# One transformer block on one core: a new order of the second product's seven partial products, five pairs of split weight tiles, and the residual added piece by piece

## The chip, the cores and the metric

The kernel runs on one core of a Trainium2 chip. The metric is the device time of one execution in microseconds (us); lower is better. A core has five engines that work through their own queues in order: TensorE (PE) multiplies matrices, VectorE (DVE) and ScalarE (ACT) do elementwise work, GpSimd (POOL) does a little of it here, and SyncE (SP) issues nearly all DMAs. Tiles lie in the on-chip memory SBUF, matmul results in the accumulator memory PSUM, which has eight banks.

## The reference

`x` is 512 rows of 2048 columns, all float32. After the attention part, the block computes a two-layer MLP with a residual:

```
x  = x + concat(headnorm(oa), headnorm(ob)) @ W_out
h2 = rmsnorm(x, g_mlp)
u  = relu(h2 @ W_up)                # W_up: 2048 x 8192
x  = x + (u * u) @ W_down           # W_down: 8192 x 2048
y  = rmsnorm(x, g_final)
```

The change lies in the lines from `W_out` on. Everything ahead of them (input projection and two kinds of attention) is left as it is.

## The kernel before, in words

**Split products.** Every float32 product is made of three matmuls (`mm3`): each operand is split into a rounded high part and a low rest, and high times high, high times low and low times high are added up. The split of a weight tile (`split`, L58 to L61) is an ACT copy that makes the high part (`wh`, L60) and a DVE subtraction that makes the low part (`wl`, L61). `hi_lo` hands out the tiles for both; there are three such pairs, handed out in turn, so a split of a fourth tile waits until PE has done with the first.

**Seven products instead of eight.** Both MLP products are computed in blocks of two by two with seven partial products each, numbered 1 to 7. Their operands are sums and differences of the blocks. On the weight side, DVE makes them in place, each from the one ahead: product 5 uses b12-b11, product 6 uses b22 minus that, product 4 uses b21 minus the operand of 6, and product 7 uses b22-b12. So product 6's operand can be made only when product 5's has been split, and so on.

**Attention output (L456 to L481).** For four column quarters `n`, PE computes `acco`; DVE adds it to `x` (L469), ACT sums the squares (L471), PE transposes, ACT scales into `hr` (L478), and `a_form` makes the seven activation operands from it and splits them into `F[p]` (tiles `fh`, `fl`).

**Up stage (32 `Unit`s).** A unit loads two raw weight tiles `wu` (pool `rw`, five buffers), makes and splits the seven operands and computes the products into three accumulators (`psa`, `psb`, `psc`), 24 matmuls a product. Products 3 and 4 of a unit run inside the next unit. After two units `store_form` makes the seven activation operands for the second product, one after each product of the loop, splits them into a staging tile `st` (two buffers) and writes them to DRAM (`ufd`).

**Down stage.** The first 30 units are read back in groups (the first of two units, seven of four). For each group and each column half `db`, four raw tiles `wd` are loaded and seven products of 12 matmuls per two units are computed, each into one of two `accd` accumulators or, for product 1, into `m`, which stays in PSUM. DVE then adds `accd` to a running sum in SBUF (L653). The residual `x` is read into four of the sums ahead of the first group and scaled there (L659 to L662). The last two units are multiplied without the seven-product scheme (`acce`), with the final norm.

**Order.** The program order is that of the code, changed by a scheduler that moves instructions of each engine by estimated times; the hardware then runs each queue strictly in the built order. SP's queue is one of them: a DMA whose buffer is not free yet holds up all DMAs behind it.

Of the kernel before, what the change touches and what calls it, by code (L numbers as in the profile page):

```python
# [8 lines left out]
F32 = mybir.dt.float32  # L9
# [26 lines left out]
def block_kernel(ctx, tc, x, g_attn, w_in, b_f, g_out_sb, g_out_fox, w_out, g_mlp, w_up, w_down, g_final, y):  # L36
# [392 lines left out]
    F = {p: tuple(form.tile([P, KC // 2, 2 * P], F32R, tag=f"f{c}{p}", name=f"f{c}{p}") for c in "hl") for p in range(1, 8)}  # L429
    xp_cm = tc.tile_pool(name="xp", bufs=1, reuse_waits="tile")  # L430
# [20 lines left out]
    for n in range(4):  # L451
# [32 lines left out]
    xp_cm.__exit__(None, None, None)  # L484
    trp_cm.__exit__(None, None, None)
    acc_cm.__exit__(None, None, None)

    v2 = cp.tile([P, TB], F32, name="v2")
    dve.tensor_reduce(v2, ss2, axis=mybir.AxisListType.X, op=ALU.add)
    dve.tensor_scalar(v2, v2, 1.0 / D, EPS, op0=ALU.mult, op1=ALU.add)  # L490
    ev = cp.tile([P, TB], F32, name="ev")
    dve.scalar_tensor_tensor(ev, v2, EPS, v2, op0=ALU.mult, op1=ALU.mult)
# [4 lines left out]
    sg_cm = tc.tile_pool(name="sg", bufs=2, reuse_waits="tile")  # L497
    sg = sg_cm.__enter__()
    ups_cm = tc.tile_pool(name="ups", bufs=1, space=PSUM, reuse_waits="tile")
    ups = ups_cm.__enter__()  # L500
    GROUPS = [(0, 2)] + [(u, 4) for u in range(2, NU - 2, 4)]
    ufd = {}
    for u0, n in GROUPS:
        t_ = {p: dp.tile([P, 2, n, 2 * P], F32, name=f"ufd{p}_{u0}") for p in range(1, 8)}
        for j in range(0, n, 2):
            ufd[u0 + j] = {p: t_[p][:, :, j:j + 2, :] for p in t_}
            ufd[u0, n] = t_
    usd = [dp.tile([P, 2, 2, NT], F32, name=f"usd{u}") for u in range(2)]

    class Unit:  # L510
        def __init__(self, u):
            self.u = u
            cols = slice(2 * u * P, 2 * (u + 1) * P)
            rows_ = w_up.rearrange("(a i p) f -> i p a f", i=2, p=P)
            if u == 0:

                self.b = [[wp.tile([P, KC // 2, P], F32, tag="wraw", name="wq") for _ in range(2)] for _ in range(1)]
                for j in range(2):
                    sp.dma_start(self.b[0][j], rows_[0][:, :, j * P:(j + 1) * P])
# [6 lines left out]
            self.A, self.B, self.C = (ups.tile([P, NT], F32, tag=c, name=f"ps{c}", bufs=n)[:, :2 * P]  # L526
                                      for c, n in (("a", 3), ("b", 2), ("c", 3)))
            if u % 2 == 0:
                hidden[0] = sg.tile([P, 2, 2, NT], F32, tag="c", name="c")
            self.pair = hidden[0]  # L530
            self.c = hidden[0][:, u % 2]

        def product(self, p):
            (b11, b12), (b21, b22) = self.b
# [14 lines left out]
            if p in (1, 6, 7):  # L549
                self.m = sg.tile([P, 2 * P], F32, tag=f"m{p}", name=f"s{p}")  # L550
# [16 lines left out]
    def store_form(p, c, dst):  # L567
        st = sg.tile([P, 2, 2, 2 * P], F32R, tag="st", name="st")
        a_form(p, c, (st[:, 0], st[:, 1]))
        sp.dma_start(dst, st.bitcast(F32))  # L570

    hidden = {}
    todo = []
    old = None
    for u in range(NU + 1):
        new = Unit(u) if u < NU else None
        for who, p in ((new, 1), (old, 4), (new, 5), (new, 6), (old, 3), (new, 2), (new, 7)):
            if who is None:
                continue
            who.product(p)  # L580
            if todo:
                store_form(*todo.pop(0))
            if p == 3 and who.u % 2 == 1 and who.u < NU - 2:
                todo += [(q, who.pair, ufd[who.u - 1][q]) for q in A_ORDER]
        old = new
    for u in range(2):
        for h in range(2):
            st = sg.tile([P, 2, NT], F32R, tag="st", name="su")
            split(st[:, 0], st[:, 1], hidden[0][:, u, h])
            sp.dma_start(usd[u][:, :, h, :], st.bitcast(F32))  # L590
    sg_cm.__exit__(None, None, None)
    ups_cm.__exit__(None, None, None)


    SUM_AT = {2: 1, 4: 5, 7: 6, 3: 2, 5: 7, 6: 4}
    UF_AT = {1: 1, 2: 5, 5: 6, 6: 2, 4: 7, 7: 4, 3: 3}
    ORDER = (1, 2, 5, 6, 4, 7, 3)
    QUADS = [[2, 3], [4, 7]]
    M = {p: form.tile([P, 2, 2, NT], F32, tag=f"fl{SUM_AT[p]}", name=f"m{p}") for p in SUM_AT}
# [3 lines left out]

    sp_ = ctx.enter_context(tc.tile_pool(name="spare", bufs=1, reuse_waits="tile"))
    dps_cm = tc.tile_pool(name="dps", bufs=2, space=PSUM, reuse_waits="tile")
    dps = dps_cm.__enter__()
    mps_cm = tc.tile_pool(name="mps", bufs=1, space=PSUM, reuse_waits="tile")
    mps = mps_cm.__enter__()
    M1 = [mps.tile([P, 2, NT], F32, name=f"m1{db}") for db in range(2)]
    uf = {}  # L610
# [5 lines left out]
    def load_b(group, db):  # L616
        u0, n = group
        rows_ = w_down[2 * u0 * P:2 * (u0 + n) * P].rearrange("(u s p) c -> s p u c", s=2, p=P)
        b = []
        for j in range(2):  # L620
            for s in range(2):
# [6 lines left out]
    def product(p, b, db, n, first):  # L628
        b11, b21, b12, b22 = b
# [10 lines left out]
        for u0 in range(0, n, 2):  # L640
            hi, lo = (w.rearrange("p (a b) -> p a b", a=2) for w in hi_lo(2 * NT))
            split(hi, lo, src[:, u0:u0 + 2, :])
            for t in range(2):
                ts = slice(t * P, (t + 1) * P)
                for u in range(2):
# [4 lines left out]
        if first and p in (5, 6):  # L650
# [4 lines left out]
    for p in ORDER:  # L655
        load_uf(p, GROUPS[0])
    for p, t0, j in ((2, 0, 0), (4, 1, 0), (7, 1, 1), (3, 0, 1)):
        for db in range(2):
            sp.dma_start(M[p][:, :, db, :], xd[2 * j + db][:, 2 * t0:2 * t0 + 2, :])  # L659
# [4 lines left out]
    ws, us, late = {}, [None, None], []  # L664
# [13 lines left out]
    def in_spare(tag):  # L678
        return lambda shape, name: sp_.tile(shape, F32R, tag=tag, name=name)

    def last_hidden(u, at_):
        t_ = at_([P, 2, 2, NT], f"us{u}")
        sp.dma_start(t_.bitcast(F32), usd[u])
        us[u] = (t_[:, 0], t_[:, 1])

    for g, group in enumerate(GROUPS):
        for db in range(2):
            if g == len(GROUPS) - 1 and db == 1:
                last_hidden(0, in_spare("us0"))
                last_weights(0, [in_spare("ws0"), in_spare("ws1")])  # L690
            b = load_b(group, db)
            for p in ORDER:
                product(p, b, db, group[1], g == 0)
                if db == 1 and g < len(GROUPS) - 1:
                    load_uf(p, GROUPS[g + 1])
    last_low = lows[0]
    last_hidden(1, in_form(1))
# [6 lines left out]
    def last_product(t, n, pool_, tag):  # L704
        ts = slice(t * P, (t + 1) * P)
        ps = pool_.tile([P, NT], F32, tag=tag, name="acce")
        for i in range(4):
            wh, wl = ws[n, i // 2]
            mm3(ps, *(h[:, i % 2, ts] for h in us[i // 2]), wh[:, i % 2, :], wl[:, i % 2, :], i == 0, i == 3)
        ins = dve.tensor_tensor(x2(t, n), x2(t, n), ps, op=ALU.add)  # L710
        junk = sp_.tile([P, NT], F32, tag="junk", name="junk3")
# [87 lines left out]
```

## Time and profile before

| | |
|---|---|
| median of 3 runs | 2134.7 us (2134.11 to 2135.95) |
| the profiled execution's own time | 2133.93 us |
| its span, first to last instruction | 2132.2 us |
| PE busy | 2088.0 us (98%) |
| DVE busy | 1572.0 us (74%) |
| ACT busy | 1019.6 us (48%) |
| mean granted clock of TensorE | 0.996 of full speed |

The profiled execution is 1.7 us longer than its span and 0.8 us below the median. Busy times of PE are made of modelled ends: a matmul of the up stage is shown 0.28 us long though the next one starts 0.12 us after it, so a wait looks shorter by the difference than it is.

### The profile page before, as it was taken

What the parts mean: (1) busy time and instruction counts of PE and PEld (TensorE: products, weight loads), DVE (VectorE), ACT (ScalarE), POOL (GpSimd) and SP (SyncE); (2) the same over time, 40 slices, a digit from 0 to 9 for tenths busy, and PEclk for the clock granted to TensorE, in tenths of its full rate; (3) what the DMA queues carried; (4) which work ended last, traced back from release to release, by engine and by line L of the source; (5) the groups of instructions that cost most, each with busy time, mean ns of one, the idle gap of its engine ahead of it and who ended that gap; (6) DMA issues with size and microseconds to landing.
All of it is one profiled execution on the core that took longest, in us unless ns stands there. A gap on an engine that the chain in (4) does not pass through costs nothing.

```text
span 2132.2 us, 29833 instructions
## 1 busy us (share of the span) xinstructions
PE 2088.0 (98%) x12084; PEld 1844.9 (87%) x12084; DVE 1572.0 (74%) x1729; ACT 1019.6 (48%) x1366; POOL 53.3 (2%) x75
## 2 busy tenths in 40 slices
PE   8999999999999999999999999999999999999998
PEld 8888887888898888999999999999778788788786
DVE  5454546665666667888888888888888878878887
ACT  5333334444445554556556556557433333333443
POOL 0000000000010000000000000000000000000004
PEclk9999999999999999999999999999999999999999
DMA  6323323323324434555656655567954564664631
GB/s 188 80 89 80 89 79 79 85 74 89 80 80 138 139 129 147 169 181 185 205 176 200 202 187 188 185 215 276 341 202 174 217 226 160 224 227 151 239 117 79
DMA packets 237354, 339.68 MB, mean 159 GB/s; under 512 B 7792, under 2 KB 150688, under 8 KB 230048
## 3 DMA queue, kind: packets, MB, share of 16 engines
q1 hardware_dynamic: 236256, 335.64, 47.7%
q8 instruction: 95, 1.56, 0.3%
q10 hardware_dynamic: 960, 2.13, 0.3%
q14 instruction: 43, 0.35, 0.0%
HBM read 272.20 MB, written 65.54 MB: 158 GB/s over the span
## 4 chain that ended last, share of the span: by engine, by line
PE 87%; DVE 6%; ACT 3%; DMA 3%; issue 1%; SPq 0%; ACTq 0%; DVEq 0%
PE accd L88 6%; PE accd L89 6%; PE accd L87 6%; PE accq L87 5%; PE accq L89 5%; PE accq L88 5%; PE psa L87 5%; PE psa L88 5%; PE psa L89 5%; PE acco L87 3%; PE acco L88 3%; PE acco L89 3%; PE psc L87 3%; PE psc L88 3%; PE accv L87 3%; PE accv L88 3%
## 5 line engine op out<-in xcount | busy, mean ns | idle before, releaser
L60 ACT CAST wh<-wd 128x1024 fp32r<-128x1024 f32 x210 | 219.7, 1054 | 338.4 <-PE accd L89 237.8
L61 DVE TENSOR_TENSOR wl<-wu,wh 128x1024 fp32r<-128x1024 f32 x220 | 267.8, 1222 | 72.5 <-ACT wh L60 72.4
L61 DVE TENSOR_TENSOR wl<-wd,wh 128x1024 fp32r<-128x1024 f32 x210 | 253.7, 1221 | 85.3 <-ACT wh L60 85.3
L60 ACT CAST wh<-wu 128x1024 fp32r<-128x1024 f32 x220 | 228.6, 1046 | 170.2 <-PE psa L88 63.1
L88 PE MATMUL accd<-wl,uf 128*128 128x512 f32 x720 | 282.5, 392 | 13.2 <-DVE wl L61 13.2
L87 PE MATMUL psa<-fh,wh 128*128 128x256 f32 x1024 | 291.3, 285 | 3.5 <-ACT s L551 2.4
L88 PE MATMUL psa<-fl,wh 128*128 128x256 f32 x1024 | 290.8, 284 | 0.0
L89 PE MATMUL psa<-fh,wl 128*128 128x256 f32 x1024 | 289.8, 284 | 0.0
L87 PE MATMUL accd<-wh,uf 128*128 128x512 f32 x720 | 279.0, 391 | 3.1 <-ACT wh L60 2.5
L89 PE MATMUL accd<-wh,uf 128*128 128x512 f32 x720 | 280.7, 390 | 0.0
L61 DVE TENSOR_TENSOR wl<-wraw,wh 128x1024 fp32r<-128x1024 f32 (+2 forms) x133 | 158.0, 1188 | 84.6 <-ACT wh L60 83.9
L60 ACT CAST wh<-wraw 128x1024 fp32r<-128x1024 f32 (+2 forms) x133 | 135.4, 1019 | 156.8 <-PE accq L88 70.3
L87 PEld LDWEIGHTS psa<-fh,wh 128*128 128x128 f32 x1024 | 197.7, 193 | 4.0 <-ACT s L551 2.6
L87 PE MATMUL accq<-hH,wh 128*128 128x512 f32 x512 | 200.9, 392 | 0.0
L89 PE MATMUL accq<-hH,wl 128*128 128x512 f32 x512 | 200.5, 392 | 0.0
L88 PE MATMUL accq<-hL,wh 128*128 128x512 f32 x512 | 200.4, 392 | 0.0
L88 PEld LDWEIGHTS psa<-fl,wh 128*128 128x128 f32 x1024 | 197.8, 193 | 0.0
L89 PEld LDWEIGHTS psa<-fh,wl 128*128 128x128 f32 x1024 | 197.4, 193 | 0.0
L88 PEld LDWEIGHTS accd<-wl,uf 128*128 128x128 f32 x720 | 135.5, 188 | 47.4 <-DVE wl L61 19.8
L87 PEld LDWEIGHTS accd<-wh,uf 128*128 128x128 f32 x720 | 135.5, 188 | 32.5 <-ACT wh L60 4.2
L89 PEld LDWEIGHTS accd<-wh,uf 128*128 128x128 f32 x720 | 135.5, 188 | 27.7
L87 PE MATMUL psc<-fh,wh 128*128 128x256 f32 x512 | 146.1, 285 | 9.3 <-ACT wh L60 7.4
(262 smaller groups left out, 4326.4 us busy)
## 6 DMA issues: line engine op xcount, KB each, us to landing
wu<-in_w_up_dram SPq DMA_DIRECT2D x63, 1024.0 KB, 6.0
wd<-in_w_down_dram SPq DMA_DIRECT2D x56, 1024.0 KB, 5.1
ufd<-st SPq DMA_DIRECT2D x105, 512.0 KB, 3.9
uf<-ufd SPq DMA_DIRECT2D x49, 1024.0 KB, 7.3
wraw<-in_w_in_dram SPq DMA_DIRECT2D x84, 512.0 KB, 3.7
wraw<-in_w_out_dram SPq DMA_DIRECT2D x32, 512.0 KB, 3.5
wraw<-in_w_in_dram SPq DMA_DIRECT2D x16, 256.0 KB, 3.0
x<-in_x_dram SPq DMA_DIRECT2D x4, 1024.0 KB, 6.7
```

Of the source, the lines that this page charges most:

```text
L60: ins = act.copy(hi, src)
L61: lows[0] = dve.tensor_tensor(lo, src, hi.bitcast(F32), op=ALU.subtract)
L87: pe.matmul(out, sh, mh, start=first, stop=False, skip_group_check=True)
L88: pe.matmul(out, sh, ml, start=False, stop=False, skip_group_check=True)
L89: pe.matmul(out, sl, mh, start=False, stop=last, skip_group_check=True)
```

## The change

It alters six things. The second product runs its partial products in the order 1, 5, 2, 6, 3, 7, 4 (before 1, 2, 5, 6, 4, 7, 3), and loads the raw tiles in the order b11, b12, b21, b22. A fourth pair of split weight tiles (`wx`, in the space of the attention output's tiles) joins from the first unit on, and a fifth (in the place of `fl3`) in the down stage. Groups have 3, 3, 4, 4... units. The first product 1 of the down stage is put ahead of the last unit's products 4 and 3, with its tiles loaded a unit earlier; for that the up stage's accumulators have two buffers each. The residual is no longer read into the sums at the start, but added to them in eight pieces from the third group on, and the first group's results are all copied by ACT. In the attention output the operands are made in the order of use (1, 5, 6, 2, 7, 4, 3, the last quarter's 4 and 3 inside the first unit), 5 and 6 in a tile of their own (`s12`), and the squares stand last. The `st` tiles come from pool `wp` (three buffers), with at most four stores a unit.

```diff
     def hi_lo(n):
+        turn[0] += 1
+        i = turn[0] % (3 + len(more_parts))
+        if i >= 3:
+            return [w[:, :n] for w in more_parts[i - 3]()]
         return [wp.tile([P, 2 * NT], F32R, tag=f"w{c}", name=f"w{c}")[:, :n] for c in "hl"]
...
-        for p in A_ORDER:
-            a_form(p, hr, [f[:, 2 * n:2 * n + 2, :] for f in F[p]])
+        s12 = xp.tile([P, 2, 2 * P], F32, tag="s12", name="s12")
+        for p in (1, 5, 6, 2, 7, 4, 3):
+            if n == 3 and p == 4:
+                break
+            a_form(p, hr, [f[:, 2 * n:2 * n + 2, :] for f in F[p]], s12)
+        for t in range(TB):
+            junk = xp.tile([P, NT], F32, tag="junk", name="junk")
+            act.activation(junk, x2[:, t, :], AF.Square, accum_out=ss2[:, t, n:n + 1])
...
-    GROUPS = [(0, 2)] + [(u, 4) for u in range(2, NU - 2, 4)]
+    GROUPS = [(0, 3), (3, 3)] + [(u, 4) for u in range(6, NU - 2, 4)]
...
-        st = sg.tile([P, 2, 2, 2 * P], F32R, tag="st", name="st")
+        st = wp.tile([P, 2, 2, 2 * P], F32R, tag="wraw", name="st")
...
-    ORDER = (1, 2, 5, 6, 4, 7, 3)
+    ORDER = (1, 5, 2, 6, 3, 7, 4)
...
-        if first and p in (5, 6):
+        if first:
             act.copy(M[p][:, :, db, :], ps)
         else:
             dve.tensor_tensor(M[p][:, :, db, :], M[p][:, :, db, :], ps, op=ALU.add)
...
+    def add_residual(p, db):
+        t0, j = {2: (0, 0), 3: (0, 1), 4: (1, 0), 7: (1, 1)}[p]
+        r = wp.tile([P, 2, NT], F32, tag="wraw", name="xr")
+        sp.dma_start(r, xd[2 * j + db][:, 2 * t0:2 * t0 + 2, :])
         for t in range(2):
-            act.mul(M[p][:, t], M[p][:, t], v2[:, 2 * t0 + t:2 * t0 + t + 1])
-    dve.tensor_tensor(M[4], M[4], M[7], op=ALU.subtract)
+            act.mul(r[:, t], r[:, t], v2[:, 2 * t0 + t:2 * t0 + t + 1])
+        dve.tensor_tensor(M[p][:, :, db, :], M[p][:, :, db, :], r, op=ALU.add)
+        if p == 7:
+            dve.tensor_tensor(M[4][:, :, db, :], M[4][:, :, db, :], r, op=ALU.subtract)
...
+        if u == NU - 1:
+            for p in ORDER:
+                load_uf(p, GROUPS[0])
+            b_first = load_b(GROUPS[0], 0)
+        if new is None:
+            second(1, b_first, 0, GROUPS[0][1], True)
...
+            if todo and i in (0, 2, 4, 5):
                 store_form(*todo.pop(0))
```

Three places show how the built order moves. The first is DVE's queue in the down stage, one column half of a group of four, in the kernel before. The four `wd` tiles here are 15770 (b11), 15772 (b21), 15774 (b12) and 15776 (b22); a row `wl` is the low half of a split, `m` a sum.

```order
L631 TENSOR_TENSOR wd_15770<-wd_15774,wd_15770 128x2048
L653 TENSOR_TENSOR m3_14171<-m3_14171,accd_15736 128x2x512
L61 TENSOR_TENSOR wl_15814<-wd_15772,wh_15813 128x1024
L637 TENSOR_TENSOR wd_15774<-wd_15776,wd_15774 128x2048
L61 TENSOR_TENSOR wl_15830<-wd_15772,wh_15829 128x1024
L61 TENSOR_TENSOR wl_15851<-wd_15770,wh_15850 128x1024
L61 TENSOR_TENSOR wl_15867<-wd_15770,wh_15866 128x1024
L633 TENSOR_TENSOR wd_15770<-wd_15776,wd_15770 128x2048
L653 TENSOR_TENSOR m2_14168<-m2_14168,accd_15812 128x2x512
L635 TENSOR_TENSOR wd_15772<-wd_15772,wd_15770 128x2048
L61 TENSOR_TENSOR wl_15888<-wd_15770,wh_15887 128x1024
L61 TENSOR_TENSOR wl_15904<-wd_15770,wh_15903 128x1024
```

The same place after the change; the tiles are 16260 (b11), 16262 (b12), 16264 (b21) and 16266 (b22), and L619, L621, L623, L625 are the operands of 5, 6, 4 and 7.

```order
L619 TENSOR_TENSOR wd_16260<-wd_16262,wd_16260 128x2048
L644 TENSOR_TENSOR m7_14308<-m7_14308,accd_16192 128x2x512
L625 TENSOR_TENSOR wd_16262<-wd_16266,wd_16262 128x2048
L61 TENSOR_TENSOR wl_16304<-wd_16260,wh_16303 128x1024
L61 TENSOR_TENSOR wl_16320<-wd_16260,wh_16319 128x1024
L644 TENSOR_TENSOR m4_14338<-m4_14338,accd_16227 128x2x512
L61 TENSOR_TENSOR wx_16339<-wd_16264,wx_16339 128x1024
L621 TENSOR_TENSOR wd_16260<-wd_16266,wd_16260 128x2048
L61 TENSOR_TENSOR wx_16354<-wd_16264,wx_16354 128x1024
L61 TENSOR_TENSOR wl_16380<-wd_16260,wh_16379 128x1024
L623 TENSOR_TENSOR wd_16264<-wd_16264,wd_16260 128x2048
L61 TENSOR_TENSOR wl_16396<-wd_16260,wh_16395 128x1024
```

Before, the operands of 6 and 4 (L633, L635) stood together ahead of the first split of 6; now the splits of 5 and 2 lie between the operands of 5 and 6, and one split of 6 between those of 6 and 4. The operand of 7 (L625), which reads b22, has moved up to the operand of 5.

The second place is DVE's queue where the attention output ends and the first unit begins, in the kernel before; `wq` and `wu` are the first unit's weights, `hr` the scaled activations.

```order
L538 TENSOR_TENSOR wq<-wu,wq 128x1024
L542 TENSOR_TENSOR wq<-wu,wq 128x1024
L61 TENSOR_TENSOR fl_5080<-hr,fh_5079 128x512
L61 TENSOR_TENSOR fl_5086<-hr,fh_5085 128x512
L61 TENSOR_TENSOR fl_5082<-hr,fh_5081 128x512
```

The same place after the change.

```order
L449 TENSOR_TENSOR s_6547<-hr 128x512
L544 TENSOR_TENSOR wq<-wu,wq 128x1024
L548 TENSOR_TENSOR wq<-wu,wq 128x1024
L61 TENSOR_TENSOR fl_5080<-hr,fh_5079 128x512
L453 TENSOR_TENSOR hr<-hr 128x2x256
```

A sum that reads `hr` now stands ahead of the two weight operands (L538 and L542 before, L544 and L548 now), which do not read it. On ACT, the four squares of the last quarter stand ahead of the `hr` rows in both programs.

The third place is PE's queue at the end of the last unit, after the change: `psa` with `fh7` is its product 7, `m1` the down stage's first product.

```order
L94 MATMUL psa_13814<-fl7_5092,wx_14037 128x256
L95 MATMUL psa_13814<-fh7_5091,wx_14037 128x256
L93 MATMUL m1_0_6582<-wh_14067,uf1_13817 128x512
L94 MATMUL m1_0_6582<-wl_14068,uf1_13817 128x512
L95 MATMUL m1_0_6582<-wh_14067,uf1_13817 128x512
```

In the kernel before, product 4 of the last unit, which adds to the same accumulator, came right behind product 7.

```order
L88 MATMUL psa_13850<-fl7_5092,wh_14058 128x256
L89 MATMUL psa_13850<-fh7_5091,wl_14059 128x256
L87 MATMUL psa_13850<-fh4_5085,wh_14090 128x256
L88 MATMUL psa_13850<-fl4_5086,wh_14090 128x256
L89 MATMUL psa_13850<-fh4_5085,wl_14091 128x256
```

Between products 7 and 4 there are now 18 matmuls of `m1`.

## Rows read from the trace of the kernel before

**Rows 1.** Stages: length, busy by engine (instructions), granted clock, DMA share, GB/s.
```profile
818.70:850.00 31.30, 27.96 (x212) 26.73 (x210) 25.42 (x31) 17.06 (x27) 0.00 (x0) 0.95 0.53 174
850.00:1470.00 620.00, 612.55 (x5077) 611.13 (x5077) 518.60 (x584) 366.33 (x497) 0.00 (x0) 1.00 0.58 190
1470.00:1550.00 80.00, 73.19 (x349) 61.24 (x348) 67.77 (x61) 44.10 (x50) 0.00 (x0) 0.96 0.90 341
1550.00:2079.70 529.70, 517.86 (x2268) 424.23 (x2267) 437.63 (x328) 202.42 (x194) 0.00 (x0) 1.00 0.55 195
```

**Rows 2.** PE by accumulator: count, ns min/median/max, first and last start (us).
```profile
L87 PE MATMUL psa<-fh,wh x1024: 278/283/415, 818.8 to 1481.9; 128*128 128x256 f32 x171
...
L87 PE MATMUL psb<-fh,wh x256: 278/283/415, 828.1 to 1472.2; 128*128 128x256 f32 x128
...
L89 PE MATMUL psc<-fh,wl x512: 279/283/415, 821.6 to 1485.2; 128*128 128x256 f32 x171
...
L87 PE MATMUL accd<-wh,uf x720: 388/389/794, 1488.1 to 2079.0; 128*128 128x512 f32 x180
...
L87 PE MATMUL acce<-ws,us x64: 389/389/389, 2079.7 to 2122.6; 128*128 128x512 f32 x64
```

**Rows 3.** Timeline of PE in the up stage: start, us, instruction.
```profile
930.22 0.28 PE L88 MATMUL psa<-fl,wh 128*128 128x256 f32 x1
930.34 0.28 PE L89 MATMUL psa<-fh,wl 128*128 128x256 f32 x1
```

**Rows 4.** Timeline of PE in the down stage, two matmuls left out.
```profile
1584.30 0.39 PE L87 MATMUL accd<-wh,uf 128*128 128x512 f32 x1
...
1584.98 0.39 PE L87 MATMUL accd<-wh,uf 128*128 128x512 f32 x1
1586.18 0.50 PE L88 MATMUL accd<-wl,uf 128*128 128x512 f32 x1 [0.81 <-DVE wl L61]
```

**Rows 5.** PE's waits, 818 to 1475: total us, times, longest.
```profile
PE psc L87 <- ACT wh L60: 7.4, 7, 1.7
PE psc L87 <- ACT fh L60: 1.8, 1, 1.8
```

**Rows 6.** PE's waits, 1475 to 1550.
```profile
PE accd L87 <- ACT wh L60: 2.5, 2, 2.0
PE psa L87 <- ACT s L551: 2.4, 1, 2.4
```

**Rows 7.** PE's waits, 1550 to 2080.
```profile
PE accd L88 <- DVE wl L61: 11.8, 14, 1.2
```

**Rows 8.** Timeline of ACT in the up stage.
```profile
1021.87 0.62 ACT L60 CAST st<-c 128x512 fp32r<-128x512 f32 x1 [4.17 <-DMA ufd<-st]
```

**Rows 9.** Tile st: DMAs from issue to landing.
```profile
DMA to landing us min/median/max: 2.6/3.9/10.4
```

**Rows 10.** DVE by line, 1550 to 2079: busy us, mean ns, idle before.
```profile
L61 DVE TENSOR_TENSOR wl<-wd,wh 128x1024 fp32r<-128x1024 f32 x188 | 227.3, 1221 | 74.2 <-ACT wh L60 74.2
L653 DVE TENSOR_TENSOR m<-m,accd 128x1024 f32<-128x1024 f32 x80 | 97.4, 1218 | 17.0 <-PE accd L89 17.0
...
L633 DVE TENSOR_TENSOR wd<-wd 128x2048 f32<-128x2048 f32 x13 | 29.8, 2292 | 0.4
```

**Rows 11.** Timeline of DVE around the wait of rows 4.
```profile
1579.36 2.29 DVE L633 TENSOR_TENSOR wd<-wd 128x2048 f32<-128x2048 f32 x1
...
1584.91 2.35 DVE L61 TENSOR_TENSOR wl<-wd,wh 128x1024 fp32r<-128x1024 f32 x2
```

**Rows 12.** Tile wd: DMAs from issue to landing.
```profile
DMA to landing us min/median/max: 3.2/5.2/14.8
```

**Rows 13.** Tile hr, 818 to 826, ACT: count, ns, first and last start.
```profile
L478 ACT ACTIVATE hr<-tr,g_rest x4: 681/690/696, 818.7 to 820.5; 128x512 f32<-128x512 f32 x4
```

**Rows 14.** Timeline of DVE as the first unit begins.
```profile
819.35 1.22 DVE L538 TENSOR_TENSOR wq<-wu,wq 128x1024 f32<-128x1024 f32 x1
...
821.70 0.69 DVE L61 TENSOR_TENSOR fl<-hr,fh 128x512 fp32r<-128x512 f32 x1
```

More of the change, by code (lines that the diff above doesn't have):

```diff
@@ L565, in product, with store_form @@
                 act.activation(self.c, self.c, AF.Square)
-    def store_form(p, c, dst):
-        st = sg.tile([P, 2, 2, 2 * P], F32R, tag="st", name="st")
+    def store_form(p, c, u):
+        st = wp.tile([P, 2, 2, 2 * P], F32R, tag="wraw", name="st")
         a_form(p, c, (st[:, 0], st[:, 1]))
[L570 to L596, printed above, removed]
-    ORDER = (1, 2, 5, 6, 4, 7, 3)
+        (g0, j0), (g1, j1) = (at_unit[u + i] for i in range(2))
@@ L598, in block_kernel @@
+    SUM_AT = dict(zip(ORDER[1:], (1, 5, 6, 2, 7, 4)))
     QUADS = [[2, 3], [4, 7]]
[L599 removed]
+    M, uf = {}, {}
     def x2(t, n):
         return M[QUADS[t // 2][n // 2]][:, t % 2, n % 2, :]
[L604 to L607, printed above, removed]
@@ L619, in load_b @@
         b = []
-        for j in range(2):
-            for s in range(2):
+        for s in range(2):
+            for j in range(2):
                 t_ = rw.tile([P, n, NT], F32, tag="rw", name="wd")
@@ L626, in load_b, with second @@
         return b
-    def product(p, b, db, n, first):
-        b11, b21, b12, b22 = b
+    def second(p, b, db, n, first):
+        b11, b12, b21, b22 = b
         if p == 5:
@@ L676, in in_form, with last_hidden @@
         return lambda shape, name: form.tile(shape, F32R, tag=f"fh{UF_AT[p]}", name=name)
[L678 to L684, printed above, removed]
+    def last_hidden(u, *tiles):
+        us[u] = []
+        for i in range(2):
+            t_ = tiles[i]([P, 2, NT], f"us{u}_{i}")
+            sp.dma_start(t_.bitcast(F32), usd[u][:, :, i, :])
+            us[u].append((t_[:, 0], t_[:, 1]))
@@ L686, in block_kernel @@
+    jobs = [lambda a=a: store_form(*a) for a in todo] + [lambda u=u, h=h: store_last(u, h) for u in range(2) for h in range(2)]
+    pieces = [(p, db) for db in range(2) for p in (2, 3, 7, 4)]
+    spare = None
     for g, group in enumerate(GROUPS):
+        last = g == len(GROUPS) - 1
         for db in range(2):
[L688 to L691, printed above, removed]
@@ L692, in block_kernel @@
-            for p in ORDER:
-                product(p, b, db, group[1], g == 0)
-                if db == 1 and g < len(GROUPS) - 1:
-                    load_uf(p, GROUPS[g + 1])
+            if last and db == 1:
+                in_w = lambda shape, name: wp.tile(shape, F32R, tag="wraw", name=name)
+                last_hidden(0, in_w, in_w)
+                last_weights(0, [lambda shape, name, i=i: spare.tile(shape, F32R, name=name) for i in range(2)])
+            b = b_first if g + db == 0 else load_b(group, db)
@@ new lines, in block_kernel @@
+            for i, p in enumerate(ORDER):
+                if g + db + i:
+                    second(p, b, db, group[1], g == 0)
+                if db == 1 and not last:
+                    load_uf(p, GROUPS[g + 1])
+                if g == 1 and jobs and i % 2 == 0:
+                    jobs.pop(0)()
+                if g > 1 and pieces and i == 2:
+                    add_residual(*pieces.pop(0))
+        if g == 1:
+            sg_cm.__exit__(None, None, None)
+            spare = ctx.enter_context(tc.tile_pool(name="spare", bufs=1, reuse_waits="tile"))
@@ L696, in block_kernel @@
     last_low = lows[0]
-    last_hidden(1, in_form(1))
+    both = form.tile([P, 2, 2, NT], F32R, tag=f"fh{UF_AT[1]}", name="us1")
+    last_hidden(1, *(lambda shape, name, i=i: both[:, i] for i in range(2)))
     def closing(db, *sums):
```

126 lines of the change are left out of this document (81 added, 45 removed).

## The prediction

> **What bounds the kernel now.** I read the stages first, then the starts of PE's matmuls, then PE's waits, and last the queues that PE waits for. In all four stages from the first unit on, PE is busy nearly throughout [rows 1]. The starts show how much is left: the first `psa` matmul begins at 818.8, the first `acce` at 2079.7 [rows 2], 1260.9 us apart. In between lie 5376 up-stage matmuls (three lines of 1024 + 256 + 512 [rows 2]) and 2520 down-stage ones (three lines of 30 units x 7 products x 2 halves x 2 row tiles = 840). At their undisturbed distance, 0.120 us [rows 3] and 0.227 us (three steps in 0.68 [rows 4]), they take 645.1 + 572.0 = 1217.1 us. So 43.8 us are lost there, and that is the ceiling: the change leaves the count and shapes of the matmuls alone, and all that comes before the attention output keeps its built order.
>
> Where they are lost follows from the length minus the busy time of each stage [rows 1], to which about 0.16 us a wait is added, since a matmul is drawn 0.16 us longer than its distance [rows 3, 4]:
>
> - Start of the up stage: 3.3 idle, and a clock of 0.95 over 31.3 us costs 1.6: about 5.
> - Up stage: 7.5 idle in 7 waits for `wh` [rows 5]: 8.6 with the correction.
> - Switch to the down stage: 6.8 idle, 3.2 for a clock of 0.96: 10.5. PE waits 2.4 for the copy of product 7's result ahead of product 4, and twice for `wh` [rows 6].
> - Down stage: 11.8 idle, nearly all in 14 waits for `wl` [rows 7]: 14.1.
>
> That makes 38; the other 5.5 are waits too short for a row and slow clock that the 1.00 rounds away.
>
> **The change, part by part.**
>
> *Order 1, 5, 2, 6, 3, 7, 4 in the down stage.* Rows 11 show the repeated wait's cause: DVE begins product 6's operand at 1579.36 (2.29 us), then adds a sum (1.22), makes 4's operand (2.28), and only at 1584.91 begins 6's low half, for which PE stands until 1586.18 [rows 4, 11]. Three operand-like steps stand in a row, and with three pairs the split ahead of them could not begin earlier. DVE has time enough in all: a block of four units needs 14 splits of 1.22, 4 operands of 2.29 and 6 sums of 1.22 [rows 10], 33.6 us against 14 x 12 x 0.227 = 38.1 of PE. After the change, from PE's end of product 7 at 0: sum 1.2, operand of 7 to 3.5, both splits of 5 to 6.0, sum of 4 (PE's end of it at 5.45) to 7.2, split of 2 to 8.4, operand of 6 to 10.7, split of 2 to 11.9, split of 6 to 13.2. PE wants that split after 4, 1, 5 and 2, at 21.8. With 8 us to spare the 14 waits go.
>
> *Groups of three, residual.* A block of three units takes PE 7 x 18 x 0.227 = 28.6 us. DVE's pieces of 1024 cost 1.22, of 512 about 0.69 (the same size in [rows 14]), an operand of 1536 about 1.75 (estimate, halfway between 1.22 and 2.29 [rows 10]): 7 x 1.91 + 4 x 1.75 + 6 x 1.22 = 27.7 us. In the first group the sums are ACT's copies, so DVE gets ahead; in the second it uses that up. Followed in its queue, the third group's first half is the tight place: its sum of 5 comes about 1.7 us after PE could use that accumulator again for 6. The residual adds 10 sums of 1.22 spread over twelve halves, 33.6 + 2.4 = 36.0 at most in most of them, inside 38.1, and takes away 8 sums of the first group. ACT's multiplications for it stay hidden: ACT is busy 202 of 530 us [rows 1]. I leave 1.7 us of loss in the down stage: 14.1 becomes 1.7, a gain of 12.4.
>
> *Fourth pair and third `st` tile in the up stage.* ACT stood 4.17 us before 1021.87 because both staging tiles were still being written to DRAM [rows 8]; such a DMA takes up to 10.4 us [rows 9]. Seven such waits precede the seven PE waits of rows 5. In the longest, 4.17 of ACT cost PE 1.7 of idle, 1.9 with the correction, so 2.3 us were covered by the weights split ahead. A fourth pair covers one product more, 24 x 0.12 = 2.9 us, so PE would wait only if ACT stands longer than 5.2; with three staging tiles and four stores a unit it stands shorter. Gain 8.6, at worst 0. The single copy tile for results 1 and 7 makes ACT wait for DVE's sum of 7; it has one product, 2.9 us, for it: nothing, at worst some tenths a unit.
>
> *Overlap at the switch.* Between product 7 and product 4 of the last unit PE now has 18 matmuls, 4.1 us, which cover the wait of 2.4 [rows 6]. After those and products 4 and 3 (2.9 each) it comes to the second `accd` product 9.9 us after product 7. DVE's queue up to that product's first low half is the operand of 7 (1.75), a sum (about 0.4), three 1024-pieces at most (3.7) and one of 512 (0.7): 6.5 us, in time. The weights and forms are loaded a unit earlier; what is late next is the third raw tile set, behind SP's loads that wait for `fh4` and `fh3`, and it has three products of 4.1 us. I leave 1.8 of 10.5: gain 8.7.
>
> *Start of the up stage.* Here the order shows no gain. `hr` is finished at 820.5 + 0.7 = 821.2 [rows 13]. Before, DVE made two weight operands from 819.35 on while it waited, and the first `fl` at 821.70 [rows 14]. Now a sum that needs `hr` stands ahead of both: 821.2 + 0.7 + 2 x 1.2 gives the first `fl` at about 824.3 to 825, where PE runs out of earlier columns at 818.8 + 36 x 0.12 = 823.1; then it waits again for the fourth `fl`, three pieces later. The better order of the forms gives about that much back. The squares have not moved (the scheduler put them ahead again). About 5 us before, about 5 after: 0, from -3 to +3.
>
> *Sum.* 12.4 + 8.6 + 8.7 + 0 = 29.7, and of the 5.5 without a row about half, 2.7: 32.4 us less. 2133.9 - 32.4 = 2101.5 for an execution like the profiled one; the median shown is 0.8 above that: 2102.3.
>
> **A rule beside it.** Rows 1 show a granted clock of 0.95 and 0.96 (of 2.4 GHz, so in part at 1.2) in the two stages whose longest waits are 1.8 to 2.4 us, and 1.00 where 14 waits are at most 1.2 [rows 5 to 7]. Each such fall costs 1.6 us (0.05 x 31.3). The two waits of about 1.8 us that I leave, at the start and in the third group, are of the size in rows 5 that goes with a fall; by the price in the rows they could add 1.6 to 3.2 us, 2104 to 2105.5, still inside the forecast. The Trainium skill, "TensorE: Matmul & The Clock Gate", "What's actually happening", says that half rate is the default state and activity releases it; rows 1 agree. By that rule alone every removed long wait gives back slow time too, which the sum already has from the rows at the switch.
>
> **The rivals.**
>
> *One of the three gains stays out (0.21).* For it speaks DVE's load of 97% in the second group (27.7 of 28.6) and 0.90 DMA share at the switch [rows 1], where the loads now come closer together. If the switch keeps its 10.5, or the up stage its 8.6, the time is about 2111; if DVE falls back by 2 to 3 us in six blocks, up to 2119.
>
> *The fourth raw tile becomes the bound: slower (0.06).* Product 4 now comes last and reads b21, whose buffer the next b22 takes; and the operand of 7, which needs b22, stands right behind that of 5. On the scale above, the second split of 4 ends 5.9 us before PE's end of product 7, the load is issued then, and PE wants the split of 5 at 10.9. Operand and split take 3.5, so PE waits once a load takes longer than 10.9 + 5.9 - 3.5 = 13.3 us. Loads take 5.2, at the longest 14.8 [rows 12]. At 15 borders it decides against the kernel when the typical load passes 13.3 + 36.7 / 15 = 15.7 us; at 17 the time would be about 2102 + 15 x 3.7 = 2158. No row comes near that in the median.
>
> *It changes nothing (0.05).* The waits move from one place to the next and end about 2132 to 2138. Against it: the lost time sits at repeated places with one cause each.
>
> **How the numbers follow.** The forecast, 2096 to 2109, has 0.64; better than that (the 5 us at the start go as well) 0.04. For 8 in 10 the range reaches into the first rival: 2095 to 2117. A difference of 0.2%, 4.3 us, is about what a measurement of this kernel can tell from none. Faster: 0.64 + 0.04 + 0.20 = 0.88; same 0.06; slower 0.06.
>
> **What would show it.** Right: no PE wait for `wl` in the steady down stage, whose start-to-start length is 572 to 576 us; no wait behind a `st` cast in the up stage; `m1` between products 7 and 4 without a gap; clock 1.00 at the switch. Wrong: PE waiting for `accd` buffers (a sum of DVE's, L644), for `wl` after L625 with DVE idle for a `wd` load, or several waits near 2 us with a lower clock. The start of the up stage should show DVE idle from about 819.3 to 821.2 and PE waiting twice for `fl`.

## The result, and the profile after

The changed kernel takes 2097.57 us (median of 4 runs, 2096.68 to 2099.45) where the kernel before took 2134.4 in the same comparison: a ratio of 0.9828, 95% interval 0.9811 to 0.9845. The forecast was 2102.3, range 2095 to 2117. The profiled execution took 2099.45 us, its span 2097.7.

The stages, with the columns of [rows 1]; the last one ends where the first `acce` begins:

```profile
818.70:850.00 31.30, 28.04 (x216) 27.23 (x214) 27.86 (x33) 18.04 (x28) 0.00 (x0) 0.95 0.62 200
850.00:1470.00 620.00, 618.77 (x5140) 617.85 (x5139) 527.03 (x596) 377.31 (x506) 0.00 (x0) 1.00 0.62 196
1470.00:1550.00 80.00, 80.00 (x376) 67.16 (x375) 60.96 (x59) 51.19 (x65) 0.00 (x0) 1.00 0.73 268
1550.00:2039.50 489.50, 487.56 (x2150) 403.07 (x2148) 431.56 (x331) 198.63 (x199) 0.00 (x0) 1.00 0.58 212
```

PE's waits from 818 to 1465 (compare [rows 5]: seven for `wh`), then from 1550 to 2050 (compare [rows 7]: fourteen for `wl`); between them there is none (compare [rows 6]):

```profile
PE psc L94 <- DVE fl L61: 1.5, 1, 1.5
PE psc L93 <- ACT wh L60: 1.2, 1, 1.2
PE psa L94 <- DVE fl L61: 0.9, 1, 0.9
PE psa L93 <- ACT s L557: 0.7, 1, 0.7
...
PE acce L93 <- DVE m L755: 1.0, 1, 1.0
PE accd L93 <- issue: 1.0, 1, 1.0
```

Three stages have almost nothing left; the start of the up stage has kept its waits. One measure makes all kernels below comparable: the distance from each PE matmul's start to the next, less 0.120 us in the up stage and 0.227 in the down stage, summed. It holds waits and slow clock alike. Worked out so from the traces, PE loses, in us (the kernels are named as in the experiments below):

| kernel | start, to 850 | up, to 1450 | switch, to 1550 | down, to `acce` | sum | median |
|---|---|---|---|---|---|---|
| before | 6.2 | 11.0 | 11.2 | 15.2 | 43.7 | 2134.4 |
| after | 5.7 | 1.5 | 0 | 1.8 | 8.9 | 2097.6 |
| up3 | 5.3 | 5.4 | 0 | 1.8 | 12.4 | 2101.7 |
| up3_seven | 5.4 | 3.1 | 0 | 1.8 | 10.2 | 2101.8 |
| up3_st2 | 5.3 | 10.8 | 0 | 1.4 | 17.5 | 2108.8 |
| down3 | 5.3 | 0 | 2.3 | 23.4 | 31.0 | 2121.2 |
| down4 | 5.6 | 2.1 | 0 | 1.4 | 9.0 | 2098.2 |
| oldorder | 5.8 | 0.8 | 0 | 0.6 | 7.1 | 2096.8 |
| nooverlap | 5.3 | 0 | 0 | 1.8 | 7.0 | 2098.1 |
| nooverlap2 | 5.7 | 0.4 | 0.6 | 1.8 | 8.5 | 2098.5 |
| before_order | 6.2 | 11.5 | 9.3 | 17.4 | 44.4 | 2135.0 |
| before_fl3 | 6.2 | 10.7 | 8.2 | 0 | 24.4 | 2116.1 |
| before_residual | 10.2 | 11.4 | 6.0 | 16.3 | 43.9 | 2133.8 |
| best | 3.0 | 0.7 | 0 | 0.6 | 4.2 | 2093.9 |

The loss fell by 34.8 us, the span of the profiled executions by 34.5: the whole gain lies in these stages. (The medians differ by 36.8, since the profiled execution of the changed kernel is the slowest of its four.) The same up stage reads 0 to 2.1 in the six kernels that build it as the changed one does, so differences of 2 us in one stage of one execution mean nothing by themselves.

### The profile page after: what moved, and what is told of

It reads as the page before. It is cut to its first block, busy times and chain, and to the rows that moved or that the text cites. A ratio compares the mean times of both kernels' runs of the same rounds, so it can differ in the third digit from the quotient of the medians.

```text
span 2097.7 us, 29846 instructions
## 1 busy us (share of the span) xinstructions
PE 2076.2 (99%) x12084; PEld 1841.3 (88%) x12084; DVE 1571.3 (75%) x1744; ACT 1034.7 (49%) x1396; POOL 50.5 (2%) x75
## 3 DMA queue, kind: packets, MB, share of 16 engines
q8 instruction: 95, 1.56, 0.3%
## 4 chain that ended last, share of the span: by engine, by line
PE 58%; DVE 1%; DMA 0%; issue 0%; ACT 0%; SPq 0%; ACTq 0%
PE accd L93 8%; PE accd L95 8%; PE accd L94 8%; PE psa L93 6%; PE psa L95 6%; PE psa L94 6%; PE psc L93 3%; PE psc L95 3%; PE psc L94 3%; PE psb L95 1%; PE psb L94 1%; PE psb L93 1%; PE m L95 1%; PE m L93 1%; PE m L94 1%; PE acce L93 1%
## 5 line engine op out<-in xcount | busy, mean ns | idle before, releaser
L61 DVE TENSOR_TENSOR wl<-wu,wh 128x1024 fp32r<-128x1024 f32 x164 | 199.6, 1222 | 45.7 <-ACT wh L60 45.4
L93 PE MATMUL psa<-fh,wh 128*128 128x256 f32 x776 | 220.3, 284 | 0.8 <-ACT s L557 0.7
L94 PE MATMUL psa<-fl,wh 128*128 128x256 f32 x776 | 220.0, 284 | 0.9 <-DVE fl L61 0.9
L60 ACT CAST wh<-wd 128x1024 fp32r<-128x1024 f32 (+1 forms) x136 | 134.7, 999 | 170.3 <-PE accd L95 108.8
L61 DVE TENSOR_TENSOR wl<-wd,wh 128x1024 fp32r<-128x1024 f32 (+1 forms) x136 | 155.6, 1154 | 41.9 <-ACT wh L60 41.5
L93 PE MATMUL accd<-wh,uf 128*128 128x512 f32 x436 | 169.7, 389 | 1.0 <-issue 1.0
L95 PE MATMUL accd<-wh,uf 128*128 128x512 f32 x436 | 169.6, 389 | 0.0
L94 PE MATMUL accd<-wl,uf 128*128 128x512 f32 x436 | 169.6, 389 | 0.0
L60 ACT CAST wx<-wd 128x1024 fp32r<-128x1024 f32 (+1 forms) x88 | 87.5, 1000 | 130.0 <-PE accd L95 78.2
L61 DVE TENSOR_TENSOR wx<-wd,wx 128x1024 fp32r<-128x1024 f32 (+1 forms) x88 | 100.8, 1153 | 23.3 <-ACT wx L60 22.9
L94 PEld LDWEIGHTS accq<-hL,wh 128*128 128x128 f32 x512 | 96.2, 188 | 19.9 <-issue 0.5
L93 PEld LDWEIGHTS accq<-hH,wh 128*128 128x128 f32 x512 | 96.2, 188 | 19.6 <-issue 0.7
```

The costliest lines, as they stand in the source:

```text
L60: ins = act.copy(hi, src)
L61: lows[0] = dve.tensor_tensor(lo, src, hi.bitcast(F32), op=ALU.subtract)
L93: pe.matmul(out, sh, mh, start=first, stop=False, skip_group_check=True)
L94: pe.matmul(out, sh, ml, start=False, stop=False, skip_group_check=True)
L95: pe.matmul(out, sl, mh, start=False, stop=last, skip_group_check=True)
```

## The experiments

**Which part emptied the down stage: the order or the pairs?** Two kernels undo one each, two add one each to the kernel before.

```diff
-    more_parts.append(lambda: parts_at(form, "fl3"))
+    more_parts.clear()
```

> The changed kernel with three pairs in the down stage, as before the change, in the new order 1, 5, 2, 6, 3, 7, 4. If the order alone takes the waits for the low half away, as the prediction worked out with three pairs, at most 1 to 2 us come back, 2097.5 to 2100. If the two further pairs did it, the waits return: 10 to 14 us, 2107 to 2112.

Measured 2121.2 us (2120.78 to 2121.78): 23.6 come back, more than either forecast. The order does not do it: with three pairs the down stage loses 23.4, more than before the change (15.2). What makes the other 8 us was not taken apart. PE's waits from 1600 to 2080, then ACT and DVE ahead of one of them, with other rows of ACT left out:

```profile
PE accd L93 <- ACT wh L60: 10.6, 11, 1.1
PE accd L94 <- DVE wl L61: 2.5, 2, 1.6
```

```profile
1665.76 1.05 ACT L60 CAST wh<-wd 128x1024 fp32r<-128x1024 f32 x1 [1.66 <-PE accd L95]
1666.85 1.22 DVE L61 TENSOR_TENSOR wl<-wd,wh 128x1024 fp32r<-128x1024 f32 x1 [1.45 <-ACT wh L60]
1668.11 2.29 DVE L619 TENSOR_TENSOR wd<-wd 128x2048 f32<-128x2048 f32 x1
1670.32 1.22 DVE L644 TENSOR_TENSOR m<-m,accd 128x1024 f32<-128x1024 f32 x1
1671.45 2.29 DVE L625 TENSOR_TENSOR wd<-wd 128x2048 f32<-128x2048 f32 x1
1673.65 3.49 DVE L61 TENSOR_TENSOR wl<-wd,wh 128x1024 fp32r<-128x1024 f32 x3
```

Operand of 5, a sum, operand of 7: 5.5 us (1668.11 to 1673.65), as long as operand of 6, sum and operand of 4 in [rows 11], now ahead of another product. The second `order` fence above shows L625 moved up to L619. The stack starts late because of the pairs: ACT's cast for the last split of product 1 waits 1.66 us for PE to give a pair back, DVE's half of that split waits for the cast, and the operand of 5, made in place in the same raw tile, comes behind it.

```diff
-    ORDER = (1, 5, 2, 6, 3, 7, 4)
+    ORDER = (1, 2, 5, 6, 4, 7, 3)
...
-        for s in range(2):
-            for j in range(2):
+        for j in range(2):
+            for s in range(2):
...
```

> The changed kernel with the second product, its load order and its tile places in the old order 1, 2, 5, 6, 4, 7, 3, and five pairs. If the order is needed, about one wait of 1 us a half block comes back: 10 to 14 us, 2107 to 2112. If five pairs are enough by themselves, since they let the splits run two half products (5.4 us) further ahead, 2097 to 2100.

Measured 2096.8 us (2095.64 to 2097.32): nothing comes back. With five pairs the order has no measurable price; the wait of 1.1 us at the third group is gone as well.

```diff
-    UF_AT = {1: 1, 2: 5, 5: 6, 6: 2, 4: 7, 7: 4, 3: 3}
-    ORDER = (1, 2, 5, 6, 4, 7, 3)
+    UF_AT = {1: 1, 5: 5, 2: 6, 6: 2, 3: 7, 7: 4, 4: 3}
+    ORDER = (1, 5, 2, 6, 3, 7, 4)
...
```

> The kernel before with only the new order 1, 5, 2, 6, 3, 7, 4 of the second product, its load order and the places that follow from the order; three pairs. By the prediction's step the waits go by the order: 10 to 12 us less, 2122 to 2125 us. By the rival, that the order only moves the stack of operand, sum, operand from product 6 to product 5: 14 to 16 waits of 1.1 us as before, and no gain: 2133 to 2140.

Measured 2135.0 us (2133.19 to 2137.34), ratio 1.0002, interval 0.9992 to 1.0011. The waits from 1550 on have changed their name, not their number:

```profile
PE accd L87 <- ACT wh L60: 12.4, 13, 1.0
PE accd L88 <- DVE wl L61: 1.6, 1, 1.6
```

```diff
...
     uf = {}
...
+    more_parts.append(lambda: parts_at(form, "fl3"))
```

> The kernel before with one thing added: a fourth pair of split weight tiles, in the place of fl3, in the down stage alone. Order, groups, residual and up stage stay. If the pairs gave the gain of the down stage and the order nothing, most of the 14 waits go: 9 to 14 us less than before, 2121 to 2126 us. If the order is needed for it, 2131 to 2135.

`hi_lo` is that of the change here. Measured 2116.1 us (2114.05 to 2116.98), 0.9908 of before (0.9891 to 0.9925): one pair of tiles more takes away 18.6 us, half of what all the changes give. Not one of the fourteen waits is left, and part of the switch, where the same splits stand, goes with them. Its stages at the switch and behind it:

```profile
1470.00:1550.00 80.00, 74.85 (x359) 62.32 (x358) 70.74 (x65) 46.01 (x50) 0.00 (x0) 0.98 0.91 342
1550.00:2050.00 500.00, 500.00 (x2207) 413.92 (x2206) 426.02 (x317) 197.19 (x189) 0.00 (x0) 1.00 0.56 204
```

```diff
-    more_parts.append(lambda: parts_at(form, "fl3"))
```

> The changed kernel without the fifth pair: four pairs in the down stage, new order. The stack of operand, sum and operand ahead of product 5's low half lasts 5.8 us and made PE wait 1.1 us with three pairs; a fourth pair lets the splits run one half product, 2.7 us, further ahead. If that is the whole story, the waits stay away and the time is 2097 to 2099 us. If the fifth pair is needed too, some of the 23.6 us that three pairs cost come back, 2102 to 2115.

Measured 2098.2 us (2096.36 to 2099.85). The fifth pair gives nothing that can be measured.

**Which part emptied the up stage: the pair, the staging tile or the spacing of the stores?**

```diff
-                more_parts.append(lambda: parts_at(hx, "hx"))
+                parts_hx = lambda: parts_at(hx, "hx")
...
-    more_parts.append(lambda: parts_at(form, "fl3"))
+    more_parts += [parts_hx, lambda: parts_at(form, "fl3")]
```

> The changed kernel with three pairs of split weight tiles in the up stage; the fourth and fifth join in the down stage. In the changed kernel ACT still stands 23 times, 41.5 us in all and 3.6 us at the longest, for the staging tiles to be written out (before: 28 times, 45.4, 4.2). If the fourth pair is what hides these waits, PE's waits of the up stage come back: 4 to 8 of them, 5 to 9 us, 2103 to 2107 us. If the third staging tile and the limit of four stores a unit did it, nothing comes back: up stage within 1 us, 2097 to 2098.5.

Measured 2101.7 us (2101.31 to 2103.14). Between the two forecasts of the two theories: the up stage loses 5.4, not 1.5 and not 11.

```diff
-            if todo and i in (0, 2, 4, 5):
+            if todo:
```

> The changed kernel with three pairs in the up stage and a store after each of seven products instead of four of them; the third staging tile stays. Three pairs with four stores lost 5.4 us in the up stage, the kernel before lost 11.0. If the spacing of the stores made the rest of that gain, 5 us more come back: 2105 to 2108 us. If not, 2101 to 2103.

This edit is made on top of up3. Measured 2101.8 us (2100.09 to 2103.41): the spacing does nothing that can be measured, beside three pairs.

```diff
-        st = wp.tile([P, 2, 2, 2 * P], F32R, tag="wraw", name="st")
+        st = sts[0].tile([P, 2, 2, 2 * P], F32R, tag="st", name="st")
...
```

> The changed kernel with three pairs in the up stage and two staging tiles, in the place that the fourth pair had; four stores a unit stay. The down stage has four pairs. If the third staging tile made the rest of the gain of the up stage, 5 us more come back than with three pairs alone: 2105 to 2108 us. If the spacing of the stores made it, 2101 to 2103.

`sts[0]` is a pool with two buffers in the place of `hx`. Measured 2108.8 us (2108.20 to 2110.67): the third staging tile is worth 7 us beside three pairs. The up stage loses 10.8, as before the change (11.0), so what else the change does there gives nothing that shows. PE's waits for `wh` from 850 to 1465, with two staging tiles and with three (up3):

```profile
PE psc L93 <- ACT wh L60: 8.6, 8, 1.4
```

```profile
PE psc L93 <- ACT wh L60: 3.9, 4, 2.0
```

ACT's waits behind them, 850 to 1460, in the kernel before, in up3_st2, in up3, and after:

```profile
ACT st L60 <- DMA ufd<-st: 45.4, 28, 4.2
```

```profile
ACT st L60 <- DMA ufd<-st: 43.4, 28, 3.9
```

```profile
ACT st L60 <- DMA ufd<-st: 27.1, 12, 5.0
```

```profile
ACT st L60 <- DMA ufd<-st: 41.5, 23, 3.6
```

The third tile more than halves the number of ACT's waits (28 to 12); their time falls from 43.4 to 27.1 us. With the fourth pair there are more again (23; perhaps since ACT then runs further ahead and meets the DMA sooner, which no run tests), and PE still waits once instead of four times.

**What emptied the switch?** The first attempt, nooverlap, put product 1 behind products 4 and 3 in the code.

```diff
-        if new is None:
-            second(1, b_first, 0, GROUPS[0][1], True)
...
         old = new
+    second(1, b_first, 0, GROUPS[0][1], True)
```

> The changed kernel with the down stage's first product put behind the last unit's products 4 and 3 instead of ahead of them; its tiles are still loaded a unit early. If the overlap gave the gain at the switch, PE waits 2.2 us again for the copy of product 7's result and the clock falls: 3 to 6 us come back, 2100.5 to 2104. If it was the earlier loads and the residual's reads taken out of the queues, at most 1 us: 2097 to 2098.5.

Measured 2098.1 us (2096.26 to 2100.41), but 12 of the 18 `m1` matmuls still stood ahead of product 4, so it tells nothing of the overlap. The second one ties them to product 3's last matmul:

```diff
+    with tc.issue_after(lasts[0].ins):
+        second(1, b_first, 0, GROUPS[0][1], True)
...
```

> The changed kernel with all 18 matmuls of the down stage's first product behind product 3 of the last unit. In the run of the first attempt the built order still had 12 of the 18 ahead of product 4, so it did not undo the overlap. If the overlap gave the gain at the switch, PE waits 2.2 us for the copy of product 7's result again, and a fall of the clock may add to it: 2 to 6 us come back, 2099.5 to 2103.5. If not, 2096.5 to 2098.5.

Measured 2098.5 us (2097.10 to 2099.50). Product 4 comes right behind product 7 again, and PE waits for the copy, but 0.5 us instead of 2.4 [rows 6]. PE and ACT at that place:

```profile
1464.80 0.28 PE L95 MATMUL psa<-fh,wx 128*128 128x256 f32 x1
1465.54 0.39 PE L93 MATMUL psa<-fh,wh 128*128 128x256 f32 x1 [0.46 <-ACT s L557]
```

```profile
1465.11 0.37 ACT L557 COPY s<-psa 128x256 f32<-128x256 f32 x1 [0.99 <-PE psa L95]
```

ACT was idle and waited for PE. In the kernel before it was not; ACT there:

```profile
1473.62 2.18 ACT L661 ACTIVATE m<-m,v 128x1024 f32<-128x1024 f32 x2
1475.71 1.04 ACT L565 ACTIVATE c<-c 128x1024 f32<-128x1024 f32 x1
1476.66 1.03 ACT L60 CAST wh<-wd 128x1024 fp32r<-128x1024 f32 x1
1477.59 0.36 ACT L551 COPY s<-psa 128x256 f32<-128x256 f32 x1
```

PE's product 7 ended at 1475.4; the copy stood in ACT's queue behind residual multiplications (L661), a square and a cast. That suggests the residual as the cause, so it was changed alone in the kernel before:

```diff
-            sp.dma_start(M[p][:, :, db, :], xd[2 * j + db][:, 2 * t0:2 * t0 + 2, :])
...
+                if g > 1 and pieces and p == 5:
+                    add_residual(*pieces.pop(0))
...
```

> The kernel before with only the residual changed: no reads and multiplications at the switch, all first sums copied by ACT, and eight pieces added from the third group on. Behind the wait of 2.4 us at the switch the trace of before shows ACT in the residual's multiplications (1.1 us each, two just ahead of the copy that PE waits for). If the residual made the loss at the switch, it falls from 11.2 us to 2 to 5, and the time to 2126 to 2130 us. If the missing overlap or the late loads made it, nothing: 2133 to 2137.

`add_residual` is that of the change, and ACT copies all first sums. Measured 2133.8 us (2130.11 to 2135.60), 0.9995 of before (0.9986 to 1.0004): no gain that can be measured. Its stages:

```profile
818.70:850.00 31.30, 26.36 (x178) 25.05 (x177) 23.26 (x28) 18.90 (x29) 0.00 (x0) 0.84 0.58 197
...
1470.00:1550.00 80.00, 74.77 (x387) 63.66 (x386) 60.81 (x56) 46.76 (x52) 0.00 (x0) 1.00 0.84 313
```

The switch loses 6.0 instead of 11.2 in this execution, but the wait for the copy stays at 2.4, so the multiplications were not what it needed:

```profile
PE psa L87 <- ACT s L551: 2.4, 1, 2.4
```

And 4.0 us more are lost at the start, at a granted clock of 0.84 instead of 0.95. Two of the pieces' multiplications were built into ACT's queue ahead of the first unit's casts; of the 4.0 us some 1.7 are longer waits, and 2.3 are matmuls 0.21 us apart instead of 0.12 (35 of them, 11 before).

```profile
820.39 1.35 ACT L664 ACTIVATE xr<-xr,v 128x512 f32<-128x512 f32 x2
821.61 1.67 ACT L60 CAST fh<-hr 128x512 fp32r<-128x512 f32 x3
```

What brings the copy in time shows beside the other kernels. In the seven with the fourth pair in the up stage (after, down3, down4, oldorder, nooverlap, nooverlap2, best) ACT begins the copy 0.2 us behind the end of product 7. In up3, up3_seven and up3_st2, the changed kernel without that pair, it begins 1.5 to 2.4 us behind it, as in the kernel before (2.2). PE and ACT in up3:

```profile
1468.37 0.28 PE L95 MATMUL psa<-fh,wl 128*128 128x256 f32 x1
1468.49 0.40 PE L94 MATMUL m<-wl,uf 128*128 128x512 f32 x1
```

```profile
1469.38 0.62 ACT L60 CAST st<-c 128x512 fp32r<-128x512 f32 x1 [1.24 <-DMA ufd<-st]
1469.91 1.05 ACT L60 CAST wh<-wu 128x1024 fp32r<-128x1024 f32 x1
1470.87 0.36 ACT L557 COPY s<-psa 128x256 f32<-128x256 f32 x1
```

ACT stood for a staging tile and then had a cast ahead of the copy, but PE went on with `m1` and lost nothing. So the fourth pair and the overlap hide the same wait, and nooverlap2 took one of them away while the other stayed. The overlap by itself, in the kernel before, was not run; nor were the groups of three units and the second buffers of the accumulators undone by themselves.

**The start of the up stage, and a faster version.** The start is the largest loss that is left. DVE there, after the change:

```profile
821.29 0.69 DVE L449 TENSOR_TENSOR s<-hr 128x512 f32<-128x512 f32 x1 [1.77 <-ACT hr L485]
821.90 1.22 DVE L544 TENSOR_TENSOR wq<-wu,wq 128x1024 f32<-128x1024 f32 x1
823.04 1.22 DVE L548 TENSOR_TENSOR wq<-wu,wq 128x1024 f32<-128x1024 f32 x1
824.17 0.68 DVE L61 TENSOR_TENSOR fl<-hr,fh 128x512 fp32r<-128x512 f32 x1
```

The kernel best is oldorder with the last quarter's forms tied behind the two weight operands, and to each other; product 5's weights are also split ahead of them:

```diff
...
+                self.weights(5)
+                self.operand(6)
+                early = self.operand(7)
+                for q in (1, 5, 6, 2, 7):
+                    with tc.issue_after(early.ins):
+                        a_form(q, hr, [f[:, 6:, :] for f in F[q]], s12)
+                    early = lows[0]
...
```

> The changed kernel in the old order of the second product, in which the trace shows no wait at the third group, and with the first unit's two weight operands ahead of the last quarter's sums on DVE, the low parts then in the order in which PE uses them. If DVE's idle stretch from 819.5 to 821.3 us is what makes PE wait for fl, the first of the two waits goes and the second shrinks from 1.7 to about 1.1: 1.7 us less than the old order alone, 2094 to 2096 us. If fl waits for ACT's casts anyway, 2096 to 2097.5.

Measured 2093.9 us (5 runs, 2093.17 to 2095.36), 0.9812 of before (0.9798 to 0.9825): below every run of the changed kernel. DVE's idle stretch is filled, the first `fl` starts at 821.22, and one wait of PE for `fl` is left, 1.0 us:

```profile
PE psc L94 <- DVE fl L61: 1.0, 1, 1.0
```

```profile
818.86 1.22 DVE L563 TENSOR_TENSOR wq<-wu,wq 128x1024 f32<-128x1024 f32 x1
819.99 1.22 DVE L567 TENSOR_TENSOR wq<-wu,wq 128x1024 f32<-128x1024 f32 x1
821.22 0.69 DVE L61 TENSOR_TENSOR fl<-hr,fh 128x512 fp32r<-128x512 f32 x1
```

The start loses 3.0 instead of the 5.8 of oldorder, 2.8 less where 1.7 was expected. Waits make 1.5 of it; the other 1.3 is slow clock, 14 matmuls 0.21 us apart in the execution of oldorder and none in this one.

## Why the prediction was right, and where its reasons were wrong

The time was right, and so were three of its four places and sizes; what it named as the cause in the largest of them was wrong.

One sum of the prediction is slightly off: 43.8 less 4.9, 8.6, 10.5 and 14.1 leaves 5.7 us without a row, not 5.5, which moves the forecast by 0.1.

**Down stage: forecast 12.4, measured 13.4, cause wrong.** The step "With 8 us to spare the 14 waits go" gave the gain to the order. Alone, the order gives nothing (before_order); the fourth pair alone gives all of it (before_fl3), and with four or five the order has no price (oldorder, down4). The step failed in two ways. It let DVE finish the first split of 6 at 13.2 us, while PE is still in the first half of product 5 (10.9 to 13.6): five pairs are in use at that moment, so the 8 us to spare are those of the pairs. With three, a split waits for PE to leave the third half product back. Down3 shows it on the same scale, with PE's end of product 7 at 1662.8: the forecast has both splits of 5 done at 6.0, but DVE begins the operand of 5 only at 5.3 and has the first split done at 12.0, where PE wants it at 10.9. And it read the operands of 6 and 4 as the fault of the order, although its own `order` rows show that the new one puts 7 beside 5: the stack is the same. The forecast came out since the program it stood for had both parts; as far as the order goes, that is luck. Its 1.7 us at the third group were measured as 1.1, at 1601.69. The Trainium skill, "Trainium Kernel Development and Optimization", "Best Practices", says that consistent bubbles can mean that SBUF ran out. The runs agree as to the tiles: fourteen waits at one place [rows 7], thirteen of them 0.97 to 1.00 us beyond the distance, were the want of one pair of tiles (before_fl3). The space for it had not run out; it lay idle.

**Up stage: forecast 8.6, measured 9.5.** Two causes that the prediction took as one: the third staging tile takes away 5.4 (10.8 to 5.4; by the times 7), the fourth pair the rest. That a four-store limit helps is not borne out (up3_seven, beside three pairs), and that ACT "stands shorter" hardly: it stands 23 times for 41.5 us, at most 3.6, where it stood 28 times for 45.4, at most 4.2, behind more cover. That PE waits only if ACT stands longer than 5.2 us was too good: ahead of 942.52 ACT stood 3.6 us, and PE lost 1.4:

```profile
942.52 0.62 ACT L60 CAST st<-c 128x512 fp32r<-128x512 f32 x1 [3.56 <-DMA ufd<-st]
...
944.14 0.39 PE L93 MATMUL psc<-fh,wh 128*128 128x256 f32 x1 [1.23 <-ACT wh L60]
```

**Switch: forecast 8.7, measured 11.2.** This term was the one that was mis-sized: nothing was left of the 1.8. The overlap, which was to cover 2.4, covers 0.6 beside the fourth pair (nooverlap2), since ACT reaches the copy in time there; with three pairs it covers the whole wait (up3). The prediction gave that wait to the overlap alone and did not see that the fourth pair takes it away too. Of the 11.2, a fourth pair in the down stage alone takes 3.0 and the residual alone 5.2, in one execution each; before_order, which adds no tile and leaves the residual as it was, reads 9.3, so parts of this size are rough.

**Start: forecast 0, measured 0.5.** The signs came as written: DVE idle from 819.5 to 821.3, the first `fl` at 824.17 (forecast 824.3 to 825), two waits for `fl`. Best shows the cause of the first by taking it away.

**The rivals.** None of the three gains stayed out, and the time moved. The fourth raw tile never decided: `wd` loads took at most 11.9 us, below the 13.3 from which PE would wait (tile `wd` after the change):

```profile
DMA to landing us min/median/max: 4.3/6.4/11.9
```

From the first `m1` at 1465.55 to the last `accd` at 2050.79 the down stage took 585.5 us with its last distance; less 48 up-stage matmuls (5.8) and 26 `acce` (5.9) that lie in it, 573.8, inside the 572 to 576 that were given as the sign.

## What to carry to other kernels

When PE waits for the same short time at the same place of every block, count first how many buffers of the late operand exist, and add one before reordering anything: one pair of tiles in space that lay idle was worth 18.6 of 36.8 us, the order written out by hand nothing. Undo each part of a change alone, and do it alone, even if the sum was forecast well: here the largest term was right for a reason that four runs refute. Two parts can hide the same wait; then undoing one of them shows little of what it does. And look at the built order of an experiment before its time is believed; the scheduler undid one of them, and put a moved piece of work ahead of something urgent in another.

## What the runs showed that was not expected

The granted clock at the start of the up stage falls in some executions and not in others behind the same waits, and a short fall costs little. After the change, and in nooverlap, PE waits twice for `fl` with gaps of 1.07 and 1.71 us beyond the distance in both; in the following stretches the clock was 0.77 and 0.95 of 2.4 GHz in the one, so in part at 1.2, and 1.00 and 1.00 in the other:

```profile
824.00:830.00 6.00, 3.54 (x17) 3.34 (x18) 6.00 (x10) 3.52 (x6) 0.00 (x0) 0.77 1.04 375
830.00:836.00 6.00, 5.37 (x43) 5.17 (x41) 5.42 (x8) 2.14 (x5) 0.00 (x0) 0.95 0.80 285
```

```profile
824.00:830.00 6.00, 4.40 (x34) 4.00 (x33) 6.00 (x9) 3.50 (x5) 0.00 (x0) 1.00 1.04 362
830.00:836.00 6.00, 4.60 (x38) 4.40 (x37) 5.83 (x8) 2.89 (x4) 0.00 (x0) 1.00 0.61 215
```

The slow matmuls, 0.21 us apart instead of 0.12, come to 13 x 0.09 = 1.2 us. But the next wait, for the copy `s` at 835, is then 0.9 instead of 1.56, and the start loses 5.7 against 5.3: 0.4 us net, not the 1.6 by which the prediction priced a fall. The start of before, with 11 such matmuls, and of before_order, with none, lose 6.2 both: the slow clock was made good by shorter waits behind it. It need not be so: before_residual, with 35 of them, loses 10.2, and no execution with its waits and a full clock is there to compare. The Trainium skill, "TensorE: Matmul & The Clock Gate", "What's actually happening", says that the number of matmuls at half rate varies from run to run of one kernel. The traces here fit that, as far as two kernels with the same program at this place can show it; each kernel has one trace.
